# TensorE in program order in three of six layers, and chain steps after every six products

## The chip, the cores and the metric

The kernel runs on one core of a Trainium2 chip. The metric is the device time of one execution in microseconds (us). TensorE (PE in the profile) multiplies matrices, VectorE (DVE), ScalarE (ACT) and GpSimd (POOL) work on the elements, and SyncE (SP) issues the DMAs. Each engine runs its own list of instructions in a fixed order and waits on semaphores for the others.

## The reference

`x` is one sequence of 512 positions with 1024 channels, in float32. Six blocks follow one another, and each adds its result to `x`:

- **A** (twice, as block 1 and block 4): `proj = rms_norm(x) @ w_in` gives queries, keys, values and a gate. Queries and keys are normed per head and rotated (RoPE). There are 8 heads, each with two score maps, masked by chunks of 64 and softmaxed; the weights are `p0 - lam * p1`. The weighted values are normed, multiplied by `silu(gate)`, and go through `w_out`.
- **B**: a gated convolution with 31 taps per channel, a layer norm, a gate and `w_out`.
- **C**: attention with low-rank queries and keys (8 heads) and `w_out`.
- **The mixers**: `rms_norm(x) @ w_in` feeds three branches: a pooling mixer, a gated linear recurrence, and a stick-breaking attention with 8 heads of 128, whose weights are `exp(log_beta + after)`, with `after` the reversed running sum of `log_sigmoid(-z)` over the keys. Each branch has its gate and its projection, and the sum goes through `w_out`.
- **FFN**: `silu(h @ w_gate) * (h @ w_up)`, then `w_down`, with 2816 hidden channels.

## The kernel before

Positions lie in four tiles of 128 (`NT`), channels in eight. Every float32 operand of a projection is split into a rounded part and a rest (`split`, `hi` and `lo`, in the type float32r), and a product is three TensorE products (`mm3`, L356): hi x hi, hi x lo, lo x hi. A product has 128 rows, usually 512 columns. Weights come through a stream (`WeightStream`): a DMA to `wr`, a ScalarE copy to `wh` (L53), and the rest `wl` by GpSimd or VectorE (L60).

Two helpers hold nearly all products. `lin_tm` (L362) gives outputs by position tile: with `tok_outer` it finishes one tile before the next. `lin_fm` (L402) gives outputs by channel tile. Both go through the products in threes (one `mm3` per step `kk`) and call `self.flow.pump()` after each three.

**The flow** (L99 to L125) decides where the smaller steps stand between the products in the program. It is a modelled clock and a heap. `mm` (L191) adds the modelled time of each product to the clock; a step is pushed with `later(us, fn)` for a modelled time in the future; `pump` emits the steps that are due; `need(cond)` emits steps, due or not, in the order of their due times, until a condition holds; `drain` emits all that is left. Steps are: `turn(t)` of a norm (transposes of a position tile of `x`, due `NORM` = 5.0 us after its scaling, L339); `turn` of a head pair (L582, transposes of queries and keys, due `A_FIRST` = 14 us or `A_TURN` after the projection); and the attention chain. A chain runs through the units (pair of heads, query tile, head): `scores` (L625), then `weights` (transposes of the attention weights, L649, due `A_WEIGHTS[0] + A_WEIGHTS[1] * n` after the scores, n keys), then `values` (L655, due `A_READY` later), and after both heads the `turn` of the output (L677, due `A_OUT` later). The next unit's scores are due `A_SPACE` after the last unit's. The mixers' chain (L1368 to L1404) is of the same form: after its scores ScalarE takes Abs, Exp, Ln (L1377 to L1379), VectorE a maximum, a scan and a subtraction (L1380 to L1385), ScalarE an Exp (L1386).

The start of the first A layer (L520 to L538) loads `x` tile by tile, runs 28 transposes of a constant on TensorE, and then calls `squares` and `norm` for the four tiles one after the other, with no TensorE work between. The first projection then asks, by `need` (L389), for its position tile's turn.

**Who sets the final order.** The kernel is written in a framework that plans each engine's order before it runs: it simulates the program and, on each engine, takes the earliest instruction in the program that is ready in its simulation. An instruction that is not ready there is overtaken by later ones. `tc.manual_schedule(engines={...})` exempts the instructions emitted in its `with` block on the named engines from this: they keep the order in which the program emits them. The kernel uses it in layer B (L1170, L1186). PSUM has eight banks of 512 float32 columns: four named `lin` for projections, two `tp` for transposes, two `sc` for scores.

Of the kernel before, what the change touches and what calls it, by code (L numbers as in the profile page):

```python
# [146 lines left out]
class K:  # L147
# [218 lines left out]
    def lin_tms(self, jobs, tok_outer=False, width=512, first=False, before_last=None, before_n=1):  # L366

        banks, per = {}, 4 if width == 256 else 2

        def go(j, t, u, w):  # L370
            opnd, nk, consume = jobs[j]
            if (j, t) not in banks:
                banks[j, t] = self.bank("lin")[:, :width]
            hi, lo = w
            for kk in range(per):
                ah, al = opnd(per * u + kk)
                s = slice(t * P, (t + 1) * P)
                last = per * u + kk == nk - 1
                self.mm3(banks[j, t], ah[:, s], al[:, s], hi[:, kk], lo[:, kk], u + kk == 0, last)
                if last:  # L380
                    consume(t, banks[j, t])
                self.flow.pump()

        order = [(j, u) for j in range(len(jobs)) for u in range(jobs[j][1] // per)]
        if tok_outer:
            w = {ju: self.ws.get([per, width]) for ju in order}
            for t in range(NT):
                if first:
                    self.flow.need(lambda: t in self.hready)  # L389
                if before_last and t == NT - 1:  # L390
                    before_last()
                for j, u in order:
                    go(j, t, u, w[j, u])
        else:
            for j, u in order:
                w = self.ws.get([per, width])
                if before_last and (j, u) == order[-before_n]:
                    before_last()
                for t in range(NT):
                    go(j, t, u, w)  # L400

    def lin_fm(self, jobs, first=False):  # L402

        banks = [[self.bank("lin") for _ in range(2)] for _ in jobs]
        w = {}

        def go(j, u, c, sl):
            opnd, nk, consume = jobs[j]
            if (j, u) not in w:
                w[j, u] = self.ws.get([4, 256])  # L410
            hi, lo = w[j, u]
            s = slice(c * P, (c + 1) * P)
            for kk in range(4):
                bh, bl = opnd(4 * u + kk)
                last = 4 * u + kk == nk - 1
                self.mm3(banks[j][c][:, sl], hi[:, kk, s], lo[:, kk, s], bh[:, sl], bl[:, sl], u + kk == 0, last)
                if last and sl.stop == S:
                    consume(c, banks[j][c])
                self.flow.pump()

        if not first:
            for j, (_, nk, _) in enumerate(jobs):
                for u in range(nk // 4):
                    for c in range(2):
                        go(j, u, c, slice(0, S))
            return

        half = S // 2
        for j, c, part in ((0, 0, 0), (1, 0, 0), (0, 1, 0), (0, 0, 1), (1, 0, 1), (1, 1, 0), (0, 1, 1), (1, 1, 1)):
            self.flow.need(lambda: all(t in self.hready for t in range(2 * part + 2)))  # L430
            for u in range(jobs[j][1] // 4):
                go(j, u, c, slice(half * part, half * part + half))
# [63 lines left out]
def units_a(ins, j):  # L496
    w, wo = ins["a_w_in"][j], ins["a_w_out"][j]
    out = []
    for p in range(4):
        c = 256 * p  # L500
        out += units_tm(w, [(c, 256), (1024 + c, 256)])
        out += units_tm(w, [(2048 + c, 256), (3072 + c, 256)])
    for half in range(2):
        for n in range(2):
            out += units_tm(wo, [(512 * n, 512)], 4 * half, 4)
    return out
# [224 lines left out]
def units_c(ins, j):  # L731
    w, wq, wkv, wo = ins["c_w_in"][j], ins["c_w_uq"][j], ins["c_w_ukv"][j], ins["c_w_out"][j]

    def heads(p):
        return units_tm(wq, [(384 * p, 384)], 0, 2) + [([1, 512], [(None, wkv[:, 512 * p : 512 * p + 512].unsqueeze(1))])]

    out = units_tm(w, [(0, 448)])
    gate = lambda p: units_fm(w, 448 + 256 * p)
    out += gate(0) + heads(0) + gate(1) + heads(1) + gate(2) + heads(2) + gate(3) + heads(3)
    for half in range(2):  # L740
        for n in range(2):
            out += units_tm(wo, [(512 * n, 512)], 4 * half, 4)
    return out
# [241 lines left out]
def units_b(ins, j):  # L985
    w, wo = ins["b_w_in"][j], ins["b_w_out"][j]
    out = []
    for c in range(0, 1024, 256):
        out += units_fm(w, 1024 + c) + units_fm(w, c)
    for c in range(0, 1024, 256):  # L990
        out += units_fm(w, 2048 + c)
    for n in range(2):
        out += units_tm(wo, [(512 * n, 512)])
    return out
# [221 lines left out]
def units_mix(ins):  # L1216
    w, wb, wo, wp = ins["w_in_2"][0], ins["w_branch_2"][0], ins["w_out_2"][0], ins["w_pool_2"][0]
    out = []
    for p in range(4):
        if p % 2 == 0:  # L1220
            out += units_tm(w, [(4096 + 256 * p, 512)])
        out += units_tm(w, [(2048 + 256 * p, 256), (3072 + 256 * p, 256)])
    for c in range(0, 1024, 256):
        out += units_fm(w, 1024 + c)

    def branch(b, more=()):
        r = []
        for c in range(0, 1024, 256):
            r += units_fm(w, 5120 + 1024 * b + c) + list(more if c == 0 else ()) + units_fm(wb[b], c)
        return r  # L1230

    out += branch(2)
    pool = lambda g: [([2, 256], [(None, wp[g].rearrange("(k p) n -> p k n", p=P))])]
    out += units_fm(w, 0) + units_fm(w, 256) + units_fm(w, 512) + pool(0) + units_fm(w, 768) + pool(1) + pool(2)
    out += branch(0, pool(3)) + branch(1)
    for n in range(2):
        out += units_tm(wo, [(512 * n, 512)])
    return out
# [341 lines left out]
def units_ffn(ins):  # L1580
    wg, wu, wd = ins["w_ffn_gate_2"][0], ins["w_ffn_up_2"][0], ins["w_ffn_down_2"][0]
    out = []
    for a, b in ((0, 6), (6, 11)):
        for c in range(a, b):
            out += units_fm(wg, 256 * c) + units_fm(wu, 256 * c)
        for n in range(2):
            out += units_tm(wd, [(512 * n, 512)], 2 * a, 2 * (b - a))
    return out
# [37 lines left out]
def build(tc, ctx, ins, out):  # L1626
    k = K(tc, ctx, ins)
    for u in (
        units_a(ins, 0), units_b(ins, 0), units_c(ins, 0), units_a(ins, 1), units_mix(ins), units_ffn(ins),
    ):  # L1630
        k.ws.add(u)
    layer_a(k, 0, 0.8 - 0.6 * math.exp(-0.3 * 0), ins["b_norm_g"][0:1, :], start=True)
    k.flow.drain()
    layer_b(k, 0, ins["c_norm_g"][0:1, :])
    k.flow.drain()
    layer_c(k, 0, ins["a_norm_g"][1:2, :])
    k.flow.drain()
    layer_a(k, 1, 0.8 - 0.6 * math.exp(-0.3 * 3), ins["norm_mix_2"][0:1, :])
    k.flow.drain()
    layer_mix(k, ins["norm_ffn_2"][0:1, :])  # L1640
    k.flow.drain()
    layer_ffn(k, out)
    k.flow.drain()
# [41 lines left out]
```

## Time and profile before

| | us |
|---|---|
| median of 3 runs | 2039.26 (2038.92 to 2047.69) |
| the profiled execution | 2043.2 |
| its span, first to last instruction | 2041.4 |
| TensorE busy | 1988.7 (97%) |
| VectorE, ScalarE, GpSimd busy | 1172.4, 996.7, 915.0 |
| TensorE's share of the chain that ended last | 81% |

The first A layer takes from 0 to about 312 us, B and C to about 757 us, the second A layer to about 1062 us, the mixers to about 1665 us, the FFN the rest. A busy TensorE is not one at its peak: the recorded ends of products are modelled and overlap, so a pitch is read from how many start in a stretch without waits. PEclk is the granted clock: 1.00 is 2.4 GHz, 0.50 is 1.2 GHz. In the rows below a line of the timeline merges neighbours of one kind and says how many (x4); a wait just before it stands in brackets with what ended it.

### The profile page before, as it was taken

What the parts mean: (1) busy time and instruction counts of PE and PEld (TensorE: products, weight loads), DVE (VectorE), ACT (ScalarE), POOL (GpSimd) and SP (SyncE); (2) the same over time, 40 slices, a digit from 0 to 9 for tenths busy, and PEclk for the clock granted to TensorE, in tenths of its full rate; (3) what the DMA queues carried; (4) which work ended last, traced back from release to release, by engine and by line L of the source; (5) the groups of instructions that cost most, each with busy time, mean ns of one, the idle gap of its engine ahead of it and who ended that gap; (6) DMA issues with size and microseconds to landing.
All of it is one profiled execution on the core that took longest, in us unless ns stands there. A gap on an engine that the chain in (4) does not pass through costs nothing.

```text
span 2041.4 us, 27224 instructions
## 1 busy us (share of the span) xinstructions
PE 1988.7 (97%) x9875; PEld 1663.7 (81%) x9875; DVE 1172.4 (57%) x2185; ACT 996.7 (49%) x2107; POOL 915.0 (45%) x812
## 2 busy tenths in 40 slices
PE   8999999999999999999999999999999999999999
PEld 6787888887898887877778888888888888888887
DVE  6677766995456656786665678747624433221321
ACT  5555646574465645555554776546423333222220
POOL 6666624993455417775535444102511223333331
PEclk9899999999999999999999999999999999999999
DMA  6122142323331323221423122322334244333331
GB/s 199 45 83 83 42 145 89 122 62 116 106 100 43 104 74 107 65 83 42 140 88 100 59 82 73 93 83 69 118 102 136 93 125 144 93 100 97 100 96 52
DMA packets 161095, 191.54 MB, mean 94 GB/s; under 512 B 15917, under 2 KB 131997, under 8 KB 160960
## 3 DMA queue, kind: packets, MB, share of 16 engines
q1 hardware_dynamic: 160960, 189.80, 29.6%
q8 instruction: 78, 1.28, 0.3%
q14 instruction: 57, 0.47, 0.1%
HBM read 177.18 MB, written 12.58 MB: 93 GB/s over the span
## 4 chain that ended last, share of the span: by engine, by line
PE 81%; DVE 6%; POOL 5%; ACT 3%; issue 2%; DMA 2%; SPq 0%; DVEq 0%; ACTq 0%; POOLq 0%
PE lin L195 71%; PE sc L195 4%; PE tp L195 3%; PE tp L303 2%; DVE wl L60 1%; POOL st L217 1%; PE lin L303 1%; POOL wl L60 1%; DMA wr<-in_a_w_in_dram 1%; POOL m L461 1%; ACT wh L53 1%; POOL m L460 1%; DVE m L580 1%; DVE st L644 0%; ACT w L638 0%
## 5 line engine op out<-in xcount | busy, mean ns | idle before, releaser
L60 POOL TENSOR_TENSOR wl<-wr,wh 128x1024 fp32r<-128x1024 f32 (+2 forms) x151 | 364.8, 2420 | 506.4 <-ACT wh L53 490.9
L53 ACT ACTIVATE wh<-wr 128x1024 fp32r<-128x1024 f32 (+2 forms) x306 | 318.6, 1044 | 376.1 <-PE lin L195 230.7
L195 PE MATMUL lin<-hh,wh 128*128 128x512 f32 (+1 forms) x928 | 350.1, 379 | 3.3 <-ACT hh L353 3.3
L195 PE MATMUL lin<-hl,wh 128*128 128x512 f32 (+1 forms) x928 | 350.1, 378 | 0.0
L195 PE MATMUL lin<-hh,wl 128*128 128x512 f32 (+1 forms) x928 | 349.2, 377 | 0.0
L195 PE MATMUL lin<-wh,hh 128*128 128x512 f32 (+2 forms) x864 | 332.9, 387 | 1.9 <-DVE sg L602 0.7
L195 PE MATMUL lin<-wl,hh 128*128 128x512 f32 (+2 forms) x864 | 329.2, 382 | 1.1 <-DVE wl L60 1.1
L195 PE MATMUL lin<-wh,hl 128*128 128x512 f32 (+2 forms) x864 | 330.1, 382 | 0.1
L60 DVE TENSOR_TENSOR wl<-wr,wh 128x1024 fp32r<-128x1024 f32 (+3 forms) x155 | 211.4, 1367 | 188.9 <-ACT wh L53 188.1
L195 PEld LDWEIGHTS lin<-hh,wh 128*128 128x128 f32 x928 | 175.7, 190 | 35.3 <-ACT hh L353 3.6
L195 PEld LDWEIGHTS lin<-hl,wh 128*128 128x128 f32 x928 | 175.9, 190 | 31.6 <-issue 0.5
L195 PEld LDWEIGHTS lin<-hh,wl 128*128 128x128 f32 x928 | 175.9, 190 | 31.2
L195 PEld LDWEIGHTS lin<-wh,hh 128*128 128x128 f32 x864 | 165.0, 191 | 29.0 <-PE tp L303 0.9
L195 PEld LDWEIGHTS lin<-wl,hh 128*128 128x128 f32 x864 | 165.2, 191 | 27.8 <-DVE wl L60 2.2
L195 PEld LDWEIGHTS lin<-wh,hl 128*128 128x128 f32 x864 | 164.8, 191 | 27.2 <-DVE hl L354 0.4
L195 PE MATMUL lin<-wh,ot 128*128 128x512 f32 x384 | 129.9, 404 | 1.2 <-ACT ot L680 1.0
L217 POOL TENSOR_TENSOR st<-st,minus_half 128x8 f32<-128x8 f32 (+4 forms) x109 | 115.5, 1061 | 7.6 <-DVE st L1159 2.3
L468 DVE TENSOR_TENSOR x<-lin,x 128x512 f32<-128x512 f32 x80 | 54.3, 687 | 102.3 <-PE lin L195 101.9
L1036 DVE SCALAR_TENSOR_TENSOR tp<-u,taps,tp 128x512 f32<-128x512 f32 x151 | 104.0, 754 | 1.1
L638 ACT ACTIVATE w<-sc,st 128x128 f32<-128x128 f32 (+3 forms) x128 | 67.0, 524 | 71.8 <-DVE st L637 71.0
L195 PEld LDWEIGHTS lin<-wh,ot 128*128 128x128 f32 x384 | 71.3, 188 | 16.1 <-ACT ot L680 2.1
L1042 POOL TENSOR_TENSOR acc<-acc,tmp 128x512 f32<-128x512 f32 x52 | 66.7, 1301 | 22.4 <-ACT tmp L1040 21.4
(321 smaller groups left out, 3814.8 us busy)
## 6 DMA issues: line engine op xcount, KB each, us to landing
wr<-in_a_w_in_dram SPq DMA_DIRECT2D x128, 256.0 KB
wr<-in_w_in_dram SPq DMA_DIRECT2D x48, 512.0 KB
wr<-in_b_w_in_dram SPq DMA_DIRECT2D x24, 512.0 KB
wr<-in_w_branch_dram SPq DMA_DIRECT2D x24, 512.0 KB
wr<-in_w_ffn_gate_dram SPq DMA_DIRECT2D x22, 512.0 KB
wr<-in_w_ffn_up_dram SPq DMA_DIRECT2D x22, 512.0 KB
wr<-in_w_ffn_down_dram SPq DMA_DIRECT2D x22, 512.0 KB
xs<-x SPq DMA_DIRECT2D x40, 256.0 KB
```

The costliest lines, as they stand in the source:

```text
L53: nc.scalar.activation(out=hi, in_=raw, func=AF.Copy)
L60: eng.tensor_tensor(out=lo, in0=raw, in1=hi.bitcast(F32), op=ALU.subtract)
L195: self.nc.tensor.matmul(out=out, lhsT=lhsT, rhs=rhs, start=start, stop=stop)
L217: self.nc.gpsimd.tensor_tensor(out=y, in0=ms, in1=self.minus_half.to_broadcast(list(ms.shape)), op=ALU.pow)
L303: self.nc.tensor.transpose(tp[:, c], a, self.ident)
L460: nc.gpsimd.tensor_tensor(out=mv, in0=rv, in1=bc(cs), op=ALU.mult)
L461: nc.gpsimd.tensor_tensor(out=m, in0=m, in1=tmp, op=ALU.add)
L468: self.nc.vector.tensor_tensor(out=xs, in0=ps, in1=xs, op=ALU.add)
L580: nc.vector.tensor_tensor(out=mv, in0=mv, in1=r.unsqueeze(2).to_broadcast([P, 8, 64]), op=ALU.mult)
L638: nc.scalar.activation(out=e[:, m, :n], in_=sc[:, :n], func=AF.Exp, bias=mx[:, m : m + 1], accum_out=sums[:, 2 * m + h : 2 * m + h + 1],)
L1036: nc.vector.scalar_tensor_tensor(out=ps, in0=tap(u[:, c], i), scalar=wc(i), in1=ps, op0=ALU.mult, op1=ALU.add)
L1042: nc.gpsimd.tensor_tensor(out=acc, in0=acc, in1=tmp, op=ALU.add)
```

## The change

In `lin_tm` and `lin_fm` the pump comes after every second step `kk`, that is after six products. The calls of both A layers and of the mixers stand in a `with tc.manual_schedule` block for TensorE; the `drain` behind each stays outside.

```diff
@@ in lin_tms @@
                 if last:
                     consume(t, banks[j, t])
-                self.flow.pump()
+                if kk % 2:
+                    self.flow.pump()
@@ in lin_fm @@
                 if last and sl.stop == S:
                     consume(c, banks[j][c])
-                self.flow.pump()
+                if kk % 2:
+                    self.flow.pump()
@@ in build @@
-    layer_a(k, 0, 0.8 - 0.6 * math.exp(-0.3 * 0), ins["b_norm_g"][0:1, :], start=True)
+    with tc.manual_schedule(engines={mybir.EngineType.PE}):
+        layer_a(k, 0, 0.8 - 0.6 * math.exp(-0.3 * 0), ins["b_norm_g"][0:1, :], start=True)
     k.flow.drain()
     layer_b(k, 0, ins["c_norm_g"][0:1, :])
     k.flow.drain()
     layer_c(k, 0, ins["a_norm_g"][1:2, :])
     k.flow.drain()
-    layer_a(k, 1, 0.8 - 0.6 * math.exp(-0.3 * 3), ins["norm_mix_2"][0:1, :])
+    with tc.manual_schedule(engines={mybir.EngineType.PE}):
+        layer_a(k, 1, 0.8 - 0.6 * math.exp(-0.3 * 3), ins["norm_mix_2"][0:1, :])
     k.flow.drain()
-    layer_mix(k, ins["norm_ffn_2"][0:1, :])
+    with tc.manual_schedule(engines={mybir.EngineType.PE}):
+        layer_mix(k, ins["norm_ffn_2"][0:1, :])
     k.flow.drain()
```

## Rows read from the trace of the kernel before

**Rows 1.** Stretches by stage: us, busy (count) of PE, PEld, DVE, ACT, POOL, PEclk, DMA
```profile
9.30:312.00 302.70, 289.96 (x1444) 238.75 (x1444) 219.86 (x484) 169.38 (x444) 183.54 (x189) 0.98 0.30 94
...
757.00:1062.00 305.00, 288.52 (x1442) 239.24 (x1441) 214.21 (x477) 160.44 (x427) 182.05 (x188) 0.98 0.27 88
1075.00:1330.00 255.00, 250.64 (x1284) 209.89 (x1284) 173.10 (x295) 154.84 (x323) 100.49 (x69) 1.00 0.26 80
```

**Rows 2.** Chain that ended last, in order of time: start us, us, what
```profile
1176.64 1.78 PE tp L195 x16
...
1380.53 284.57 PE lin L195 x1250
```

**Rows 3.** TensorE's groups by shape, second A layer: xcount | busy us, mean ns
```profile
L195 PE MATMUL lin<-wh,hh 128*128 128x512 f32 x256 | 103.7, 406 | 0.7 <-DVE sg L602 0.7
...
L195 PE MATMUL tp<-vt,wT 128*128 128x128 f32 x160 | 23.9, 280 | 1.5 <-ACT wT L652 1.5
...
L195 PE MATMUL sc<-ks,qs 128*128 128x512 f32 x32 | 10.4, 410 | 1.5 <-ACT w L638 1.5
...
L303 PE MATMUL tp<-ident,x 128*128 128x128 f32 x24 | 3.4, 272 | 0.0
```

**Rows 4.** The same groups, mixers' attention (1075 to 1330 us)
```profile
L195 PE MATMUL lin<-wh,hl 128*128 128x512 f32 x183 | 72.9, 398 | 0.0
...
L195 PE MATMUL tp<-wT,vt 128*128 128x128 f32 x160 | 21.6, 275 | 0.6 <-ACT wT L1393 0.6
...
L195 PE MATMUL lin<-yh,wl 128*128 128x512 f32 x16 | 6.2, 390 | 0.0
```

**Rows 5.** TensorE's longest wait (timeline), and a stretch behind it
```profile
54.04 1.09 PE L303 MATMUL lin<-ident,m 128*128 128x128 f32 x4 [3.86 <-DVE m L580]
...
52.00:59.00 7.00, 4.96 (x14) 4.13 (x15) 3.23 (x7) 1.82 (x6) 6.58 (x7) 0.53 0.01 4
```

**Rows 6.** Waits of VectorE in the second A layer: total us, times, longest
```profile
DVE sc L636 <- PE sc L195: 23.1, 19, 3.6
```

**Rows 7.** Timeline of the start, TensorE and VectorE: start us, us, what
```profile
9.52 0.50 PE L195 MATMUL lin<-wh,hh 128*128 128x512 f32 x1 [0.46 <-ACT hh L353]
...
29.71 0.60 PE L303 MATMUL tp<-ident,x 128*128 128x128 f32 x4
...
23.22 1.40 DVE L338 SCALAR_TENSOR_TENSOR x<-x,st,gain 128x512 f32<-128x512 f32 x2
...
25.74 1.28 DVE L354 TENSOR_TENSOR hl<-tp,hh 128x512 fp32r<-128x512 f32 x2
```

**Rows 8.** Products (L195) in two stretches of the start: us, PE busy (count)
```profile
9.30:27.50 18.20, 13.81 (x53) 9.52 (x54) 1.00 0.81 248
9.30:29.80 20.50, 16.11 (x62) 11.14 (x62) 1.00 0.80 246
```

**Rows 9.** Timeline, two score products with 512 keys and the last VectorE step after each
```profile
295.52 0.63 PE L195 MATMUL sc<-ks,qs 128*128 128x512 f32 x2
...
298.37 0.75 DVE L645 SCALAR_TENSOR_TENSOR w<-w,st 128x512 f32<-128x512 f32 x1
...
849.45 0.73 PE L195 MATMUL sc<-ks,qs 128*128 128x512 f32 x2
...
859.85 0.99 DVE L645 SCALAR_TENSOR_TENSOR w<-w,st 128x512 f32<-128x512 f32 x1
```

**Rows 10.** Timeline of the mixers, two scores with 512 keys and the Exp after each
```profile
1160.71 0.40 PE L195 MATMUL sc<-qkt,yh 128*128 128x512 f32 x1
...
1166.91 0.63 ACT L1386 ACTIVATE l<-l 128x512 f32<-128x512 f32 x1
...
1198.83 0.39 PE L195 MATMUL sc<-qkt,yh 128*128 128x512 f32 x1
...
1211.45 0.62 ACT L1386 ACTIVATE l<-l 128x512 f32<-128x512 f32 x1
```

**Rows 11.** Timeline, VectorE's scaling of m beside weight splits, and alone
```profile
1201.57 2.89 DVE L1342 TENSOR_TENSOR m<-m,st 128x512 f32<-128x512 f32 x1 [0.62 <-POOL st L217]
...
1214.00 0.68 DVE L1342 TENSOR_TENSOR m<-m,st 128x512 f32<-128x512 f32 x1
...
1201.51 7.58 POOL L60 TENSOR_TENSOR wl<-wr,wh 128x1024 fp32r<-128x1024 f32 x3
```

## The prediction

> **What bounds the kernel now.** The page comes first. TensorE is busy for 1988.7 us of the 2041.4 us span, and 81% of the chain that ended last is TensorE, so a change counts only by TensorE time that it adds or removes. Next come the stretches by stage [rows 1]: the first attention layer from its first product, the second one, and the mixers' attention. They last 302.7, 305.0 and 255.0 us. What TensorE must do in them is a count of instructions times a pitch. The pitch is read where nothing waits [rows 2]: 284.57 us for 1250 products of 512 columns is 0.2277 us each, and 1.78 us for 16 narrow ones of 128 columns is 0.111 us each.
>
> The second attention layer [rows 3]: 768 products of the projections (three forms of 256) and 192 of the output projection are 960 x 0.2277 = 218.6 us. 160 value products and 80 + 64 + 32 + 24 transposes (weights, heads, outputs, next layer's input) are 360 x 0.111 = 40.0 us. The score products are 32 each of 128, 256, 384 and 512 columns, the two ends at 0.111 and 0.228 us and the others between, 20.2 us. Together 278.8 us, so 26.2 of the 305.0 us are waits and half clock. The first attention layer has the same work and four more transposes, 279.2 us, and so loses 23.5 of its 302.7 us. The mixers' attention [rows 4]: nine forms of 512-column products with 183, 182, 182, 88, 88, 88, 16, 16 and 16, that is 859, are 195.6 us; 316 narrow ones are 35.1 us; scores (24 of each width) and some setup take 17.1 us. That is 247.8 us, and 7.2 us are lost. All of it: 26.2 + 23.5 + 7.2 = 56.9 us.
>
> Where such a loss arises is in the waits [rows 5]. A first head transpose stands 3.86 us for m from VectorE, and behind it 7 us run at a granted clock of 0.53, which costs 3.3 us more. The Trainium skill, in "TensorE: Matmul & The Clock Gate" (HAM oscillation), says that a pause of TensorE brings its clock down and the next work starts slow; this row agrees, and by that rule a long wait costs about twice its length. The reverse happens too: VectorE stands 23.1 us in the second attention layer for score products that TensorE has not yet issued [rows 6]. The two engines wait for each other because each has a fixed order and the two orders were planned with other durations than the chip's.
>
> **The change, part by part.** Inside the three wrapped layers TensorE takes its instructions as the program emits them. Nothing is added or removed on any engine, and no DMA: what moves is where the chain steps stand among the products. Layers B, C and the FFN keep the planner's order; there, only the point at which a step is emitted moves, and the planner still moves it on. I put that at nothing, since their chains are small beside the products (the bound is about 2 us either way, one step's wait per layer).
>
> *The start of the first layer* (a loss). All four turns of the first norm are due at the same modelled time, because nothing advances the flow's clock between them. `need` therefore emits all eight transpose groups before the first product. In the trace the first product starts at 9.52 us, while the last group of transposes starts at 29.71 us [rows 7]. Under the program's order the first product comes behind that last group. The group needs the fourth tile's scaling, done at 23.22 + 1.40 = 24.6 us, and a PSUM bank that VectorE frees at 25.74 + 1.28 = 27.0 us [rows 7]. So the first product starts at about 27.5 us. Before 27.5 us the old kernel had done 53 products [rows 8]: 53 x 0.2277 = 12.1 us that now come later. TensorE has stood long by then, so I add one stretch at half clock, 3.4 us (half of 7 us, rows 5). Together +15.5 us. The bounds: with free banks a start at 25 us and no half clock, about +10; with the old 29.8 us, 62 products [rows 8] and the half clock, 14.1 + 3.4 = +17.5.
>
> *What the old order lost* goes: -56.9 us at most, as counted above.
>
> *What the new order loses instead.* A step that is not ready when TensorE arrives now holds every product behind it. Each is emitted a fixed modelled time after the step that feeds it, and the modelled clock charges 512/2400 = 0.2133 us for a product that takes 0.2277 us, so the real distance is 1.067 times as long. A pump after six products instead of three rounds it up by 0.7 us on average (half of six products), not by 0.35 us. For the attention weights with 512 keys: 3.5 + 0.0065 x 512 = 6.8, times 1.067, plus 0.7 is 8.0 us. Against this stands the reaction, from the end of the scores to the end of the last VectorE step. A quick one [rows 9]: 295.52 + 0.63 = 296.15 to 298.37 + 0.75 = 299.12, 3.0 us; it is 5 us early. A slow one [rows 9]: 849.45 + 0.73 = 850.18 to 859.85 + 0.99 = 860.84, 10.7 us; it would hold TensorE for 2.7 us. The bounds are no late unit, 0, and all 32 units of a layer, 86 us. I take the end near the quick row, three late units or 8 us a layer, because the slow reactions come from a VectorE that stands in line, not one that is full: 214.2 of 305.0 us busy [rows 1], with 23.1 us of it waiting for scores that now come sooner [rows 6].
>
> In the mixers the distance is (3.5 + 0.007 x 512) x 1.067 + 0.7 = 8.3 us. A quick reaction [rows 10]: 1160.71 + 0.40 to 1166.91 + 0.63, 6.4 us; a slow one: 1198.83 + 0.39 to 1211.45 + 0.62, 12.9 us, which is 4.6 us late. Bounds 0 and 32 x 4.6 = 147 us; I take two late units, 9 us, near the quick row again. In all 8 + 8 + 9 = 25 us.
>
> A rule that speaks against the small end: in the slow unit VectorE's scaling of m takes 2.89 us, in another place 0.68 us, while GpSimd runs weight splits for 7.58 us [rows 11]. The Trainium skill, "SBUF — State Buffer" (SBUF: two separate sides), says that a VectorE operation with two SBUF inputs and a GpSimd operation that reads SBUF exclude each other. The trace agrees, and no order of TensorE removes it; by the rule the mixers' late units stay many, which is the slower rival below.
>
> The sum, on the profiled execution's 2043.2 us: +15.5 - 56.9 + 25 = -16.4, 2026.8 us. The median of the runs, 2039.26 us, lies 3.9 us below that execution, so I forecast 2023 us.
>
> **The rivals.**
>
> *The chains hold TensorE (slower).* One mechanism: in the mixers and both attention layers the weights steps come up before VectorE, ScalarE and GpSimd have finished them, and what used to be shifted behind products now stops them. For it speak the slow rows above and that VectorE, ScalarE and GpSimd are busy 53 to 70% in the attention layers [rows 1] with steps that depend on each other in turn. Against it: six products per pump lengthen every distance. With six late units in each of the three layers it costs 2 x 6 x 2.7 + 6 x 4.6 = 60 us: 2039 + 15.5 - 56.9 + 60 = 2058 us. It decides the sign from 41 us of such waits (56.9 - 15.5).
>
> *Nothing waits.* All distances hold, 0 instead of 25 us: 1998 us. For it speaks the quick row's 5 us of room; against it the slow ones.
>
> *The start doesn't suffer.* The first products somehow get ahead of the fourth tile's transposes: 2023 - 15.5 = 2007 us. Against it stands the emission order itself.
>
> *Another engine sets the pace.* Each pair's chain is bound by VectorE and GpSimd, the wait only changes its name, and the time stays within 10 us of 2039 us. For it speaks the 70% of VectorE, against it that the work without waits is 57 us shorter.
>
> **How the numbers follow.** Forecast 0.34, slower rival 0.26, another engine 0.18, nothing waits 0.15, start spared 0.07. What this measurement can tell from no change is about 0.5%, 10 us, so faster means below 2029 us. The forecast's own range is 2008 to 2038 us: of its 0.34, 0.25 lies below 2029 and 0.08 within. With the two cheap rivals (0.22) and a little of the fourth, faster is 0.49. Within 0.5%: 0.08, most of the fourth and a little of the slower one, 0.24. Slower: 0.27. The range that should hold 8 in 10 goes from 1994 us (the start at its low bound with no late unit) to 2052 us (late units of some 55 us).
>
> **What would show it.** The first product at 25 to 30 us, behind the eighth group of transposes, and half clock there: the start's term. In the two attention layers, order on TensorE with scores ahead of their pair's later products, VectorE's wait for scores far below 23 us, and a second attention layer of some 287 us (305 - 26 + 8): the middle term. TensorE's waits for m, w and l above 25 us in sum, or a mixers' attention longer than 257 us: the slower rival. The prediction is wrong in kind if the second attention layer is not shorter than 300 us.

## The result, and the profile after

The changed kernel takes 2094.68 us (median of 5 runs, 2092.62 to 2098.37), against 2042.3 us of the kernel before in the same session: ratio 1.0259, 95% interval 1.0241 to 1.0278. The forecast was 2023 us; the sign is wrong. Compared below are the two profiled executions, 2041.4 and 2090.8 us of span, 49.4 us apart.

The head of the page and the shares of its chain; before, TensorE was busy 1988.7 us and had 81% of the chain:

```profile
PE 1993.4 (95%) x9875; PEld 1665.5 (80%) x9875; DVE 1155.8 (55%) x2185; ACT 1008.5 (48%) x2107; POOL 903.3 (43%) x812
...
PE 74%; DVE 8%; POOL 7%; ACT 5%; issue 4%; DMA 2%; SPq 0%; POOLq 0%; ACTq 0%; DVEq 0%
```

TensorE does the same 9875 instructions, but the chain that ended last runs more often through the other engines: TensorE now stands for them. The stretches, with the columns of [rows 1] (the first and second attention layer from their first product, the mixers' attention, and what follows it):

```profile
26.50:324.00 297.50, 276.95 (x1394) 229.37 (x1393) 197.55 (x460) 157.27 (x416) 172.58 (x174) 0.99 0.25 80
772.00:1075.00 303.00, 279.92 (x1418) 232.05 (x1417) 211.47 (x478) 163.16 (x426) 176.51 (x187) 0.99 0.26 85
1088.00:1340.00 252.00, 231.51 (x1167) 192.85 (x1165) 151.16 (x281) 148.92 (x312) 101.86 (x75) 0.97 0.24 75
1340.00:1430.00 90.00, 83.43 (x360) 68.06 (x359) 39.71 (x55) 44.69 (x58) 7.16 (x6) 0.96 0.27 76
```

In the third stretch TensorE runs 1167 instructions in 252 us, where before it ran 1284 in 255 us. For a comparison that doesn't depend on where a stretch is cut, all kernels of this study are measured at the same marks of the timeline: the first product; the start of the last output product of each attention layer and of C; the start of the last product of the mixers (with `mh` or `ml`). Stage lengths in us; from there to the start of the last FFN product it is 362.1 us in all of them. The lengths come from one profiled execution of each kernel, the medians from all. Stages with the same code differ by up to 3 us between kernels, and in two places by more: A2 of g2 is 318.5 where the changed kernel has 313.0, and the mixers of e1 are 625.1 where e3, e4, g3 and h1 have 615.0 to 616.6. (The profiled executions of e1, g1 and g2 are 4.7, 5.4 and 3.2 us above their medians.) So a gain is read from the medians first, and the stages say where it lies. The planner can also move work across a border.

| kernel | median | ratio to before (95%) | first product | A1 | B+C | A2 | mixers |
|---|---|---|---|---|---|---|---|
| before | 2042.3 | | 9.5 | 315.5 | 441.4 | 308.0 | 610.4 |
| changed | 2094.7 | 1.0259 (1.0241 to 1.0278) | 26.9 | 334.5 | 437.3 | 313.0 | 639.9 |
| e1 pump only | 2038.8 | 0.9977 (0.9968 to 0.9986) | 9.9 | 313.5 | 438.6 | 298.4 | 625.1 |
| e2 order only | 2107.7 | 1.0304 (1.0283 to 1.0326) | 26.7 | 348.0 | 434.3 | 317.6 | 641.9 |
| e3 mixers planned | 2069.9 | 1.0125 (1.0110 to 1.0140) | 26.7 | 335.4 | 436.6 | 314.3 | 615.2 |
| e4 order in A2 only | 2048.8 | 1.0029 (1.0019 to 1.0038) | 9.7 | 311.4 | 438.6 | 314.5 | 615.6 |
| f1 A_OUT 12 | 2077.0 | 1.0166 (1.0151 to 1.0181) | 26.2 | 328.2 | 437.5 | 302.5 | 640.6 |
| f2 first turns apart | 2088.0 | 1.0218 (1.0201 to 1.0235) | 9.7 | 330.0 | 436.9 | 314.3 | 639.7 |
| f3 convolution between | 2088.1 | 1.0218 (1.0203 to 1.0233) | 26.9 | 334.8 | 438.8 | 316.1 | 630.2 |
| f4 gates later | 2089.1 | 1.0223 (1.0208 to 1.0238) | 26.3 | 336.6 | 438.2 | 315.8 | 630.4 |
| g1 mixers' distances | 2086.5 | 1.0216 (1.0201 to 1.0232) | 26.7 | 337.4 | 438.6 | 314.6 | 633.2 |
| g2 mixers' rests on VectorE | 2084.6 | 1.0205 (1.0184 to 1.0227) | 26.9 | 337.0 | 438.7 | 318.5 | 625.7 |
| g3 order in A2, both longer | 2045.6 | 1.0008 (0.9999 to 1.0017) | 9.6 | 311.6 | 438.5 | 311.5 | 615.0 |
| g4 all mends | 2066.5 | 1.0111 (1.0097 to 1.0125) | 9.7 | 322.0 | 438.6 | 312.4 | 626.8 |
| h1 order in A2, A_OUT 12 | 2039.2 | 0.9979 (0.9971 to 0.9988) | 9.6 | 311.9 | 439.6 | 303.0 | 616.6 |
| h2 planned, g2's rests | 2024.7 | 0.9914 (0.9900 to 0.9927) | 9.8 | 312.1 | 439.0 | 298.8 | 606.9 |
| h3 fixed, A layers' rests on VectorE | 2077.6 | 1.0171 (1.0157 to 1.0185) | 26.3 | 327.4 | 436.8 | 304.4 | 639.4 |
| h4 mends that gained | 2051.2 | 1.0043 (1.0030 to 1.0057) | 9.8 | 321.1 | 437.5 | 303.0 | 621.1 |
| i1 planned, no rests on GpSimd | 2011.5 | 0.9844 (0.9830 to 0.9857) | 9.7 | 305.7 | 437.7 | 294.3 | 606.5 |
| i2 fixed, no rests on GpSimd | 2053.1 | 1.0042 (1.0030 to 1.0055) | 9.7 | 320.3 | 438.1 | 305.8 | 621.2 |

So the 49.4 us of the two profiles are 19.0 in A1, -4.1 in B and C, 5.0 in A2 and 29.5 in the mixers. What TensorE lost between the same marks (A1 from its first product): us idle before its instructions, then us at half clock.

| kernel | A1 | A2 | mixers |
|---|---|---|---|
| before | 14.2, 10.2 | 16.5, 10.2 | 5.8, 0 |
| changed | 20.5, 6.8 | 23.1, 6.8 | 27.1, 20.5 |
| e1 pump only | 11.9, 13.7 | 11.5, 6.8 | 10.5, 20.5 |
| i1 planned, no rests on GpSimd | 8.1, 3.4 | 7.1, 3.4 | 3.1, 0 |
| i2 fixed, no rests on GpSimd | 21.6, 3.4 | 16.7, 3.4 | 12.4, 13.7 |

In A2 the idle time grew by 6.6 us, and 3.4 us less of half clock gave some 1.7 back: 4.9 of the 5.0 us. In the mixers idle time grew by 21.3 us, and 20.5 us at half clock cost some 10: 31.5 where 29.5 were measured. (That half clock costs half its length is an estimate; it holds where TensorE is busy.) The loss is TensorE standing, and its clock behind that.

**The start.** TensorE's timeline (start us, us, what), then stretches as above. The first product comes behind the last of the transposes, and the stretch around it runs at half clock, for the most part while TensorE stands:

```profile
24.89 2.33 PE L303 MATMUL tp<-ident,x 128*128 128x128 f32 x8 [3.82 <-issue]
26.87 0.77 PE L195 MATMUL lin<-wh,hh 128*128 128x512 f32 x1
...
13.00:30.10 17.10, 9.23 (x32) 7.03 (x33) 14.09 (x23) 9.75 (x19) 7.35 (x13) 0.51 0.71 220
```

**The waits.** TensorE's waits in the second attention layer (total us, times, longest). The kernel before, 757 to 1062 us, the six longest:

```profile
PE sc L195 <- ACT w L638: 3.7, 4, 1.5
PE lin L303 <- DVE qs L354: 3.6, 1, 3.6
PE tp L303 <- ACT tp L662: 1.5, 3, 0.7
PE tp L303 <- DVE og L675: 1.5, 1, 1.5
PE tp L195 <- ACT wT L652: 1.5, 3, 0.7
PE tp L303 <- DVE w L645: 1.4, 2, 1.1
```

The changed kernel, 772 to 1075 us (program lines stand two further down), and what VectorE waits for scores there, which answers to [rows 6]:

```profile
PE tp L303 <- DVE og L677: 9.7, 4, 3.2
PE lin L303 <- DVE qs L354: 3.8, 1, 3.8
PE sc L195 <- ACT w L640: 3.7, 5, 1.3
PE tp L303 <- ACT tp L664: 3.0, 3, 1.1
PE tp L303 <- DVE w L647: 2.0, 2, 1.1
PE lin L303 <- DVE m L582: 0.8, 1, 0.8
...
DVE sc L638 <- PE sc L195: 16.9, 10, 5.5
```

The old waits are nearly all still there, under the same names: 3.6 for qs became 3.8, 3.7 for sc (whose bank ScalarE's step on w frees) stayed 3.7, 1.4 for w became 2.0. The program's order does not remove them. Beside them stands a larger one, 9.7 us for og where there were 1.5. In the first attention layer one old wait did go: the 3.86 us for m of [rows 5] is now (26.5 to 324 us)

```profile
PE lin L303 <- DVE m L582: 1.1, 1, 1.1
```

The changed kernel's mixers, attention (1088 to 1340 us) and the gates behind it (1340 to 1380 us); before, the attention's waits came to 4.4 us in all, 2.1 of them for m:

```profile
PE tp L303 <- ACT l L1388: 9.5, 8, 2.4
PE lin L303 <- DVE m L1344: 7.0, 4, 2.3
PE tp L195 <- ACT wT L1395: 2.7, 3, 1.8
...
PE sc L195 <- POOL b L1451: 3.9, 1, 3.9
PE sc L195 <- ACT b L1450: 2.7, 1, 2.7
```

One late unit of the mixers shows the mechanism, and answers to [rows 10, 11] (timeline: start us, us, what; rows between these are left out). Its score products end at 1223.10; GpSimd begins three weight rests; VectorE's scaling of m, 0.68 us when alone, takes 2.40 and the scan behind it 3.40; the Exp ends at 1232.36, 9.3 us after the scores. The program has placed the transposes 6.9 us after the scores (TensorE arrives at 1229.99), so they stand 2.42 us, and all products behind them too. Half clock follows (second fence, stretch as above):

```profile
1222.70 0.40 PE L195 MATMUL sc<-qkt,yh 128*128 128x512 f32 x1
...
1224.68 8.44 POOL L60 TENSOR_TENSOR wl<-wr,wh 128x1024 fp32r<-128x1024 f32 x3
1225.24 2.40 DVE L1344 TENSOR_TENSOR m<-m,st 128x512 f32<-128x512 f32 x1
1227.57 3.40 DVE L1384 TENSOR_TENSOR_SCAN rl<-rl,l 128x512 f32<-128x512 f32 x1
...
1231.73 0.63 ACT L1388 ACTIVATE l<-l 128x512 f32<-128x512 f32 x1 [2.03 <-DVE l L1387]
1232.41 0.66 PE L303 MATMUL tp<-ident,l 128*128 128x128 f32 x4 [2.42 <-ACT l L1388]
```
```profile
1235.00:1245.20 10.20, 7.43 (x33) 6.76 (x33) 6.12 (x16) 5.76 (x16) 1.88 (x2) 0.51 0.29 91
```

In the kernel before such a unit reacted as slowly (12.9 us), but the planner had put products between [rows 10].

### The profile page after: what moved, and what is told of

The parts are those of the page before. It is cut to its first block, busy times and chain, and to the rows that moved or that the text cites. A ratio compares the mean times of both kernels' runs of the same rounds, so it can differ in the third digit from the quotient of the medians.

```text
span 2090.8 us, 27222 instructions
## 1 busy us (share of the span) xinstructions
PE 1993.4 (95%) x9875; PEld 1665.5 (80%) x9875; DVE 1155.8 (55%) x2185; ACT 1008.5 (48%) x2107; POOL 903.3 (43%) x812
## 4 chain that ended last, share of the span: by engine, by line
PE 74%; DVE 8%; POOL 7%; ACT 5%; issue 4%; DMA 2%; SPq 0%; POOLq 0%; ACTq 0%; DVEq 0%
PE lin L195 65%; PE sc L195 4%; PE tp L303 2%; PE tp L195 2%; POOL st L217 2%; DVE wl L60 1%; POOL wl L60 1%; ACT wh L53 1%; PE lin L303 1%; DMA wr<-in_a_w_in_dram 1%; DVE rl L1384 1%; DVE st L639 1%; POOL m L462 1%; POOL m L463 1%; ACT w L640 1%
## 5 line engine op out<-in xcount | busy, mean ns | idle before, releaser
L195 PE MATMUL lin<-hh,wh 128*128 128x512 f32 (+1 forms) x928 | 350.6, 379 | 0.0
L195 PE MATMUL lin<-hh,wl 128*128 128x512 f32 (+1 forms) x928 | 349.3, 377 | 0.0
L195 PE MATMUL lin<-hl,wh 128*128 128x512 f32 (+1 forms) x928 | 348.8, 376 | 0.0
L195 PE MATMUL lin<-wh,hh 128*128 128x512 f32 (+2 forms) x864 | 338.1, 391 | 0.1
L195 PE MATMUL lin<-wh,hl 128*128 128x512 f32 (+2 forms) x864 | 326.5, 378 | 0.0
L195 PE MATMUL lin<-wl,hh 128*128 128x512 f32 (+2 forms) x864 | 325.5, 377 | 0.0
L195 PEld LDWEIGHTS lin<-hh,wl 128*128 128x128 f32 x928 | 175.6, 189 | 31.8
L195 PEld LDWEIGHTS lin<-hl,wh 128*128 128x128 f32 x928 | 175.6, 189 | 31.4 <-issue 0.5
L195 PEld LDWEIGHTS lin<-hh,wh 128*128 128x128 f32 x928 | 175.4, 189 | 31.2 <-issue 0.5
L195 PEld LDWEIGHTS lin<-wh,hl 128*128 128x128 f32 x864 | 164.0, 190 | 30.4
L195 PEld LDWEIGHTS lin<-wh,hh 128*128 128x128 f32 x864 | 164.8, 191 | 23.9 <-DVE sg L814 0.3
L195 PEld LDWEIGHTS lin<-wl,hh 128*128 128x128 f32 x864 | 164.4, 190 | 23.7 <-DVE wl L60 0.3
L195 PE MATMUL lin<-wh,ot 128*128 128x512 f32 x384 | 132.0, 406 | 0.0
L217 POOL TENSOR_TENSOR st<-st,minus_half 128x2 f32<-128x2 f32 (+4 forms) x109 | 113.1, 1039 | 5.0
L195 PEld LDWEIGHTS lin<-wh,ot 128*128 128x128 f32 x384 | 72.8, 190 | 15.4
L592 POOL CAST qs<-qs 64x512 fp32r<-64x512 f32 x64 | 46.2, 721 | 69.5 <-DVE qs L354 60.6
```

What stands on the lines that cost most here:

```text
L195: self.nc.tensor.matmul(out=out, lhsT=lhsT, rhs=rhs, start=start, stop=stop)
L217: self.nc.gpsimd.tensor_tensor(out=y, in0=ms, in1=self.minus_half.to_broadcast(list(ms.shape)), op=ALU.pow)
L592: nc.gpsimd.tensor_copy(out=q[v, :, m_], in_=q[u, :, m_])
```

## The experiments

**Which half of the change, and which layer.** The texts set off below are what was expected before each run. e1 leaves the three `with` blocks out, e2 takes the pump's condition out, e3 leaves the block around `layer_mix` out, e4 those around `layer_mix` and the first `layer_a`.

```diff
-                if kk % 2:
-                    self.flow.pump()
+                self.flow.pump()                      # e2
...
-    with tc.manual_schedule(engines={mybir.EngineType.PE}):
-        layer_mix(k, ins["norm_ffn_2"][0:1, :])
+    layer_mix(k, ins["norm_ffn_2"][0:1, :])           # e1, e3, e4
```

> The pump after six products alone, every layer's TensorE order left to the planner. Theory (the fixed order costs the time, because a step that is not ready holds the products behind it): the planner moves a step on wherever it stands, so the time stays at the kernel before, 2035 to 2049 us. Rival (the pump after six thins the steps out, the chains end later and the layers with them): most of the 52 us is here, 2075 us or more.

> The fixed order in the three layers alone, the pump after every three products as before. Theory (fixed order): the loss stays, and as each step comes up to 0.35 us earlier than with six it may grow: 2090 to 2110 us. Rival (pump): the loss goes with the pump, 2050 us or less.

> The changed kernel with the mixers' TensorE order given back to the planner; both attention layers keep the program's order. Theory (the stage marks of the two traces: 37 of the 52 us arise between the mixers' first product and their last): 2094.7 - 37 = about 2058 us, 2050 to 2066. Rival (the mixers inherit their loss from a weight stream or from VectorE's order that the attention layer before leaves behind): above 2080 us.

> The program's order in the second attention layer alone, the pump after six. Theory (stage marks: this layer gained 1.6 us, the forecast's 26 us of old waits were replaced by as many new ones): 2034 to 2046 us, a second attention layer of 301 to 305 us in the window that starts at its first product. What the forecast said of this layer (-26 + 8): about 2024 us and a layer of 287 us.

Measured: 2038.8, 2107.7, 2069.9, 2048.8 us. The pump after six products gains 4.3 us by itself and 13 under the fixed order; the rival that blamed it is out. The fixed order costs 10.0 us in A2 (e4 - e1), 21.1 in A1 (e3 - e4) and 24.8 in the mixers (changed - e3): 55.9 us, which with the pump's -4.3 makes the result. e3 and e4 missed their ranges by 4 and 3 us: stage marks of the changed kernel against the kernel before had put 37 us on the mixers and next to nothing on A2. By the table the pump's gain in A2 (308.0 to 298.4, e1) had hidden what the order costs there (298.4 to 314.5, e4).

**Single places mended, the fixed order kept.**

```diff
-A_OUT = 8.5
+A_OUT = 12.0                                                        # f1
-        self.flow.later(NORM, lambda: self.turn(t))
+        self.flow.later(NORM + self.apart * t, lambda: self.turn(t))  # f2: 5.5 in the first norm, else 0
             for p in range(4):
+                if p == 3:
+                    conv(0)                                         # f3: its weights moved too
                 project(p)
-            flow.later(10.0, lambda: Chain(flow).add([lru_gate(i) for i in range(8)]))
+            flow.later(18.0, lambda: Chain(flow).add([lru_gate(i) for i in range(8)]))  # f4
```

> The changed kernel with A_OUT = 12.0 instead of 8.5: the transposes of a finished output pair stand 3.5 modelled us later in the program, in both attention layers. Theory (a fixed order costs what a step's reaction is longer than its distance, and the distance can be mended): the transposes of og stop waiting, 8.1 us in the first and 9.7 us in the second attention layer, with half clock behind three of them 18 to 28 us in all; about 2072 us, 2066 to 2080. Rival (the chain of a pair is bound by VectorE and GpSimd, and the wait goes on to the next step): 2088 us or more.

> The changed kernel with the four turns of the first norm due 5.5 modelled us apart, so that the program has the first tile's products ahead of the second tile's transposes. Theory (the start's term, +15.5 us, is an order of emission): the first product at about 9.5 us again, and all but some 3 us of the term returned, since the products of tile 0 now wait for the stream's fourth weight: 2094.7 - 12 = 2083 us, 2079 to 2087. Rival (the start is bound by the first weights and by the norm of the four tiles, whatever the order): 2091 us or more.

> The changed kernel with the first of the mixers' four blocks of convolution products (48 products, 10.9 us) placed between the head pairs 2 and 3 instead of behind pair 3. Theory (the waits of the mixers' attention arise where need(attended(1)) empties the heap ahead of time and the distances shrink to 0 to 3 us): the cluster of waits and half clock between 1200 and 1250 us, 9 us more than before, goes: about 2085 us, 2080 to 2089. Rival (every unit of that chain reacts too slowly, wherever it stands): 2092 us or more, and the waits for l, wT and m keep their sum of some 19 us.

> The changed kernel with the chain of the recurrence's eight gates due 18 instead of 10 modelled us after the attention. Theory (the first gates stand 2.7 and 3.9 us for the block matrix that is loaded and split just before, and half clock follows, 9 us in all): about 2086 us, 2082 to 2090, and no wait of TensorE for b. Rival (the wait returns in the scans, which need all eight gates, or in the branches that merge them): 2092 us or more.

Measured: 2077.0, 2088.0, 2088.1, 2089.1 us. f1 does what its theory says: 6.3 us in A1, 10.5 in A2. f4 too: no wait of TensorE between 1335 and 1430 us is left, and it gains 5.6 us in the median (9.5 by the marks of the mixers). f2 gains 6.7 us where 12 were expected, and misses its range by 1 us. Its first product stands at 9.7 us again, but the program's order then holds tile 0 for its last weights (TensorE's waits, 9 to 60 us):

```profile
PE lin L196 <- DVE wl L60: 5.4, 3, 2.9
PE lin L196 <- DVE st L579: 1.8, 1, 1.8
```

Until the fourth piece of the weight stream has its rest (23.3 us), f2 starts 19 products, all that tile 0 can do in the program's order. The kernel before, whose fourth rest came at 23.2 us, starts 38 until then, so its planner had put products of another tile there. f3 gains 6.5 us in the median (9.7 by the marks of the mixers), inside its range, but not for its reason: the waits for l, m and wT are 11.3, 6.3 and 2.1 us, 19.7 after 19.2, as the rival said. What went is half clock (20.5 us of it between 1088 and 1380 us before the edit, 6.8 after it) and most of the wait for b (6.6 to 1.5 us: the block matrix is ready at 1357.6 instead of 1360.4 us, the first gate starts at 1355.6 instead of 1355.8). So the emptied heap is not what makes the units late; the reaction is.

**The distances, and who makes the reaction slow.**

```diff
-SB_TURN = 6.0
+SB_TURN = 9.0                   # g1
-SB_WEIGHTS = (3.5, 0.007)
+SB_WEIGHTS = (6.0, 0.007)       # g1
-SB_POOL = 1.0
+SB_POOL = 0.0                   # g2
```

> The changed kernel with longer distances in the mixers' chain: SB_WEIGHTS 6.0 + 0.007 n instead of 3.5 + 0.007 n, and SB_TURN 9.0 instead of 6.0. Theory (the units wait because their distance is 0 to 1 us shorter than their reaction, 9.5 us for l and 7.0 us for m, with 17 us at half clock behind them): most of 16.5 + 8.5 us goes, 2074 us, 2067 to 2082. Rival (the chain is bound by VectorE, ScalarE and GpSimd together, so a longer distance meets a longer reaction): 2088 us or more, with waits for l and m still above 12 us.

> The changed kernel with the weights' rests (wl) computed by VectorE instead of GpSimd in the mixers' attention (SB_POOL 0.0 instead of 1.0). Theory A (a reaction is slow where VectorE's step runs beside GpSimd's split: a scan over 512 took 3.4 us in four units and 1.2 to 1.3 us in the others): the scans stay at 1.3 us, the scaling of m near 0.7 us, the waits for l and m shrink, about 2080 us, 2072 to 2088. Theory B (VectorE's line is what counts, and each rest adds 1.2 us to it): the waits for l and m grow, 2095 us or more.

Measured: 2086.5 and 2084.6 us. g1 falls between its theories, and its waits say why (TensorE, 1050 to 1345 us; og belongs to A2 and is left out):

```profile
PE tp L195 <- ACT wT L1395: 5.0, 4, 1.8
PE sc L195 <- DVE l L1387: 4.7, 2, 4.0
PE tp L303 <- DVE yl L354: 3.8, 2, 3.5
...
PE lin L303 <- DVE m L1344: 1.7, 3, 0.8
PE tp L303 <- ACT l L1388: 1.6, 2, 1.3
```

The waits for l and m fell from 16.5 to 3.3 us, those for l, m and wT with the two new ones only from 19.2 to 16.8: with longer distances more units are open than `sc` and `tp` have banks (two each), and scores and transposes wait for a bank instead. g2 goes at the reaction itself. VectorE's groups in the mixers' attention (1085 to 1345 us: xcount | busy us, mean ns), first the changed kernel with GpSimd's rests in its last line, then g2:

```profile
L1344 DVE TENSOR_TENSOR m<-m,st 128x512 f32<-128x512 f32 x16 | 16.6, 1039 | 4.2 <-POOL st L217 4.1
L1384 DVE TENSOR_TENSOR_SCAN rl<-rl,l 128x512 f32<-128x512 f32 x8 | 15.8, 1981 | 5.2 <-ACT l L1381 5.2
...
L1387 DVE TENSOR_TENSOR l<-sc,rl 128x512 f32<-128x512 f32 x8 | 5.5, 690 | 0.2
...
L60 POOL TENSOR_TENSOR wl<-wr,wh 128x1024 fp32r<-128x1024 f32 x31 | 78.4, 2548 | 43.0 <-ACT wh L53 42.6
```
```profile
L60 DVE TENSOR_TENSOR wl<-wr,wh 128x1024 fp32r<-128x1024 f32 x37 | 45.6, 1236 | 16.0 <-ACT wh L53 15.2 <-PE tp L195 0.4
...
L1344 DVE TENSOR_TENSOR m<-m,st 128x512 f32<-128x512 f32 x16 | 11.0, 686 | 2.6 <-POOL st L217 2.5
L1384 DVE TENSOR_TENSOR_SCAN rl<-rl,l 128x512 f32<-128x512 f32 x8 | 9.8, 1219 | 0.9 <-ACT l L1381 0.9
...
L1387 DVE TENSOR_TENSOR l<-sc,rl 128x512 f32<-128x512 f32 x8 | 5.5, 684 | 0.1
```

Theory A holds: the 512-wide scan goes from 1981 to 1219 ns, the scaling of m from 1039 to 686, the waits for m vanish and those for l fall from 9.5 to 5.3 us, although VectorE now does 32 rests more. (Its expectation counts four slow scans in the changed kernel; the trace has three of eight, 2.92, 3.40 and 3.40 us.)

**All mends, and the second attention layer alone.** g4 joins f1 to f4 and g1, with A_WEIGHTS (4.5, 0.0065); g3 is e4 with A_OUT 12.0 and that A_WEIGHTS in its layer; h1 is e4 with A_OUT 12.0 there and nothing else; h4 joins f1 to f4 and g2.

```diff
-A_WEIGHTS = (3.5, 0.0065)
+A_WEIGHTS = (4.5, 0.0065)       # g4, and in the second layer of g3; not in h1, h4
```

> The program's order in the second attention layer alone, as before, and in that layer A_OUT 12.0 instead of 8.5 and A_WEIGHTS 4.5 + 0.0065 n instead of 3.5 + 0.0065 n. Theory (waits are distances that are too short): the 9.7 us for og, the 2.0 us for w and a stretch of half clock go, so 2048.8 - 13 = 2036 us, 2030 to 2041: this layer under the program's order is then about as good as under the planner's, and the forecast's 26 us of old waits are still not won. Rival (the fixed order has no room at all, whatever the distances): 2046 us or more.

> The changed kernel with all mends together: turns of the first norm apart, A_OUT 12.0 and A_WEIGHTS 4.5 + 0.0065 n, the first convolution block between the pairs 2 and 3, SB_WEIGHTS 6.0 + 0.007 n and SB_TURN 9.0, the gates after 18. Theory (each place's wait is its own): the gains add up, 17.6 + 6.7 + 6.5 + 5.6 as measured one by one, about 20 of the mixers' distances and 3 of the attention weights: 2035 us, 2025 to 2048. Rival (the engines behind the chains set the pace and the mends take the same time away): 2055 us or more.

> The program's order in the second attention layer alone, with A_OUT 12.0 there and the weights' distance as it was. Theory (the weights' longer distance took back what the outputs' distance gave: that layer lasted 302.4 us with A_OUT alone and 311.5 us with both): 2048.8 - 11 = about 2038 us, 2033 to 2042, no better than the pump alone (2038.8). Rival (a mended order wins back the old waits of this layer): 2030 us or less.

> The changed kernel with the mends that gained alone: turns of the first norm apart, A_OUT 12.0 with the weights' distance as it was, the first convolution block between pairs 2 and 3, the gates after 18, and the mixers' rests on VectorE. Theory (each wait has its own place): 2094.7 - 17.6 - 6.7 - 6.5 - 5.6 - 10.1 = 2048 us, 2042 to 2056, about the kernel before and still not below it. Rival (what is mended in one place returns in another): 2062 us or more.

Measured: 2045.6, 2066.5, 2039.2, 2051.2 us. g4 went with its rival, and g3 came to the edge of its own: A2 lasts 311.5 and 312.4 us, where A_OUT alone gave 302.5. Dropping the longer A_WEIGHTS brought it back (h1 303.0, h4 303.0). By itself (g3 to h1) that distance took 6.4 us in the median and 8.5 by the marks of A2: there TensorE's idle time is 20.0 us in g3 and 14.1 in h1 (for og 4.1 against 1.3, for a `tp` bank that ScalarE's L664 frees 3.1 against none), its half clock 10.2 and 3.4. h1 and h4 came out as expected. With the best distances found, A2 in program order is level with the pump alone (2039.2 against 2038.8), and the whole kernel still 12 us above it.

**GpSimd relieved, under both orders.** h2 and h3 move the weights' rests to VectorE in one place each; i1 and i2 in all three layers, i1 with the planner's order everywhere, i2 with the fixed order and f1 to f4.

```diff
-SB_POOL = 1.0
+SB_POOL = 0.0                   # h2, i1, i2
-A_POOL = 0.3
+A_POOL = 0.0                    # h3, i1, i2
```

> The pump after six products, every order the planner's, and the weights' rests of the mixers' attention on VectorE (SB_POOL 0.0). Theory (GpSimd's rests slow VectorE's steps, and the planner's order had hidden that behind products): 2034 to 2042 us, the same as the pump alone (2038.8). Rival (GpSimd's rests cost time under either order): 2030 us or less, as the program's order gained 10 us from it.

> The changed kernel with no weight rests on GpSimd in the attention layers (A_POOL 0.0 instead of 0.3: 11 of 39 rests of a layer move to VectorE). Theory (the waits that both orders have in these layers, for og, qs, m and w, come from GpSimd's line of rope and norm factors, in which 11 rests of 2.4 us stand): the waits shrink by a third or more in both layers, 2076 to 2086 us. Rival (VectorE's line sets them, and takes 11 x 1.2 us more): 2094 us or more.

> The pump after six products, every order the planner's, and no weight rests on GpSimd in the mixers' attention and both attention layers (SB_POOL 0.0 and A_POOL 0.0). Theory (GpSimd's line is late under either order, and the planner hides only a part): below the 2024.7 us of the kernel that has the mixers' rests alone on VectorE, by 5 to 15 us: 2010 to 2020 us. Rival (in the attention layers the planner's order had already hidden GpSimd's rests behind products, and VectorE's longer line costs as much as it gives): 2021 to 2030 us.

> The program's order in all three layers with the mends that gained, and no weight rests on GpSimd in these layers. Theory (of h3's 17 us some 10 were the waits for og, which A_OUT 12.0 has already won): 2051.2 - 7 = 2044 us, 2036 to 2050, 20 us or more behind the planner's order with the same rests. Rival (without GpSimd's late steps the fixed distances hold, and the order that was forecast pays at last): 2025 us or less.

Measured: 2024.7, 2077.6, 2011.5, 2053.1 us. h2 refutes its theory: the planner had not hidden GpSimd's rests, they cost 14.1 us under its order too (e1 to h2). h3 gains 17.0 us under the fixed order, and the longest step there, og, is mostly mended by it (9.7 to 2.5 us in A2, 8.1 to 2.5 in A1); the waits for sc and w are not, they are 4.9 and 3.7 us in A2. Since f1 had won og's wait, i2 is no better than h4, and misses its range by 3 us. i1 is in its range and beats both kernels: 0.9844 of the kernel before. It and i2 do the same arithmetic with the same rests on VectorE (i2 has f1 to f4 besides), and are 41.6 us apart: 14.6 in A1, 11.5 in A2, 14.7 in the mixers. TensorE's idle time alone differs by 13.5, 9.6 and 9.3 us there. The longest of TensorE's waits in A2 (745 to 1055 us), i1 and then i2:

```profile
PE lin L195 <- DVE st L578: 3.1, 1, 3.1
PE lin L195 <- ACT ot L682: 1.1, 2, 0.6
PE tp L303 <- ACT tp L664: 1.1, 3, 0.4
```
```profile
PE sc L196 <- ACT w L641: 4.9, 4, 1.3
PE tp L304 <- DVE w L648: 4.0, 3, 1.4
PE lin L196 <- DVE st L579: 3.1, 1, 3.1
PE tp L304 <- DVE ot L684: 1.8, 2, 0.9
PE tp L304 <- DVE og L678: 1.3, 1, 1.3
```

The 3.1 us for st stands in both; it has taken the place of the wait for qs. What i2 has besides are single chain steps, each up to 1.4 us late at a place fixed in advance; under the planner's order none of these for sc, w and og holds TensorE.

## Why the prediction was wrong

The mechanism was the one of the slower rival: chains hold TensorE. But that rival's 2058 us missed too, as it kept the -56.9 us below, and part of what the fourth rival said (the wait only changes its name) came with it. Step by step:

- *What the old order lost goes, -56.9.* This step failed. It took all the loss for a conflict of two planned orders that the program's order would end. Instead TensorE's idle time in A1, A2 and the mixers rose from 36.5 to 70.7 us and its half clock from 20.4 to 34.1. In A2 the term says -26.2 and, with the new waits, 18 us shorter; the program's order alone cost 10.0 us there (e4 against e1), and the stretch of 305.0 us is still 303.0, so by its own test (not shorter than 300 us) the prediction was wrong in kind. Of the old waits in A2, that for qs is 3.6 to 3.8 us long about 39 us into the layer under either order. Without GpSimd's rests it changes its name, again under either order: 3.1 us for st, 35 us into the layer (h3, i1, i2). Both steps of VectorE free a bank of `lin`, so it is a late result and no conflict of orders. The waits for sc and w are smaller under the planner's order (1.6 and 1.5 us in e1, none in i1), but under the fixed one they stay even without GpSimd's rests (4.9 and 4.0 in i2): for them the planner's order was the better one.
- *The size of that term* was too large as well. In the three stretches of [rows 1] the waits come to 33.5 us, and 20.4 us at half clock cost some 10: about 44 of the 56.9. The rest is in the count of work: A2 without its idle time and half of its half clock takes 283 to 288 us in every kernel here, not 278.8.
- *The start, +15.5.* The first product was right (27.5 forecast, 26.9 measured). From 9.3 to 30 us TensorE starts 7 products (L195) where it started 62, so it is 55 x 0.2277 = 12.5 us behind, as the term says. From 30 to 60 us it starts 128 against 96 and gets 7.3 us back: the wait for m and the half clock of [rows 5] don't come. Here the old loss did go. 23 products, 5.2 us, are left, and f2 won 6.7 back. The half clock lasted 17.1 us and not 7, but only the last 3.4 of it lie behind the first product.
- *New waits, +25.* Right where it looked and blind elsewhere. For the mixers' weights it said 9 us and 9.5 came (eight units late by little, not two by 4.6; in the unit shown the distance was 6.9 us, not 8.3). For the attention weights it said 16, and 5.8 came, of which 4.0 were there before. It priced no other step: og 17.8 us, m 7.0, `tp` banks in attention 6.2, wT 2.7, the gates' matrix 6.6, and the half clock behind them. It should have put a distance against a reaction for every kind of step in the program. Its sign for the slower rival, waits for m, w and l above 25 us, came to 24.1 (8.8, 5.8 and 9.5).
- *The pump at nothing.* That was said of B, C and the FFN, within 2 us. In the whole kernel the pump gains 4.3 us by itself (e1), and by the marks B and C are 2.8 us shorter there; the cause was not traced.
- *The rule against the small end* was heard and then outweighed by the quick rows. g2 shows its size: 762 ns per 512-wide scan and 353 ns per scaling of m, on the mean. The Trainium skill, "SBUF — State Buffer" (SBUF: two separate sides), has a VectorE operation with two SBUF inputs and a GpSimd operation that reads SBUF exclude each other. The trace agrees: both steps return to one duration (1219 and 686 ns) once GpSimd has no rests, and the subtraction behind the scan (L1387), which reads one operand from PSUM, takes 690 and 684 ns. How much of the 27 us from e1 to i1 is this, and how much GpSimd's shorter line, was not separated.
- *Smaller slips.* VectorE is busy 73% of the first attention layer, so 53 to 70% should be 53 to 73%. The bounds of 86 and 147 us charge all 32 units with rows of 512 keys, which 8 of them have.

VectorE's wait for scores fell from 23.1 to 16.9 us, as the middle term said, and that was no gain: TensorE is the bound, and it waited more.

Open: why og comes late again under the longer A_WEIGHTS, and how the new waits of the mixers divide between distances that are too short and reactions that are too slow: g1 mends the one and g2 the other, each alone, and their sum was not measured.

## What to carry to other kernels

A wait in a trace is not the order's until it is shown to be gone under another order; list the waits by releaser first, and ask whether that engine is late under any order. Fixing the bound engine's order trades a planner that can put work in front of a late step for a constant distance: too short it stalls, too long it runs out of banks, so shorten the slow reaction first (here 27 us by taking one kind of step off GpSimd, e1 to i1) and leave the order alone. Price every kind of step that the fixed order passes, not the one that the trace shows largest.

## What the runs showed of the hardware

A weight's rest of 128 x 1024 takes 2548 ns on the mean on GpSimd (changed kernel) and 1236 ns on VectorE (g2). In the changed kernel's mixers' attention, VectorE's three 512-wide scans that begin while GpSimd has a rest take 2.92, 3.40 and 3.40 us, the five others 1.22 to 1.23. The three scalings of m that begin so take 2.40 to 2.89 us; two during which a rest begins take 0.67 and 0.68, like the eleven beside none (0.68 to 0.70). The subtraction of the same width that reads PSUM (L1387) takes 0.69 us in the three cases beside a rest and in the five others.

So the 32 rests that g2 gives to VectorE cost it 32 x 1.236 = 40 us of its own time, and made the kernel 10 us faster under the fixed order and 14 under the planner's: VectorE was not full (151 of 252 us busy), and steps in the chain's path got shorter.
